# Turning the local-attention gates by a transposing DMA instead of on TensorE, in a hybrid retention and sliding-window layer

## The chip, the cores and the metric

The kernel runs on one core of one Trainium2 chip. The metric is the device time of one execution in microseconds (us). Before the change it is 714.54 us, the median of three runs (714.14 to 716.06).

## The reference

One layer of a decoder, for one sequence of 2048 tokens with 1024 channels, all in float32. One input projection gives the queries, keys, values and gates of two groups of heads: a retention (four heads, in chunks of 128 tokens) and a sliding-window softmax attention (eight heads, window 128). Each group's output is multiplied by SiLU of its gate, the two are put side by side and projected back:

```python
def reference(x, norm_w, w_in, ret_norm_w, q_norm_w, k_norm_w, sinks, rel_bias, w_out):
    h = rms_norm(x, norm_w).astype(x.dtype)
    proj = jnp.einsum('bsd,de->bse', h, w_in).astype(jnp.float32)
    rq, rk, rv, rg, sq, sk, sv, sg = jnp.split(proj, offsets, axis=-1)
...
    ro = ro * jax.nn.silu(rg)
...
    so = so * jax.nn.silu(sg)
    mixed = jnp.concatenate([ro, so], axis=-1).astype(x.dtype)
    x = x + jnp.einsum('bse,ed->bsd', mixed, w_out)
```

What matters here is the gating, `so * silu(sg)`, and that its result is the stationary operand of the output projection, for which it must lie with the channels on the partitions.

## The kernel before, in words

The 2048 tokens are 16 chunks of 128, taken as eight pairs `p` of an even chunk (row 0) and an odd chunk (row 1). Every projection is done as one level of a Strassen-like scheme: the input is cut into quarters (two rows of tokens, two halves of the inner dimension), and seven products `m` = 1 to 7 of sums and differences of quarters give the four quarters of the result. So there are four stages, each of 7 x 8 products: two for the queries, keys and values, one for the gates (`W3`, `B3`, L1421 to L1423), one for the output projection (`W4`, `B4`, L1424 to L1426). A product is 12 matmuls of 128 x 512, because each operand is split into a high part that TensorE's fast float32 mode keeps whole and a low rest (`split`, L493: the high part by ScalarE, the rest by VectorE): high by high, high by low, low by high, for four slices of the inner dimension.

The products of a stage go in the order of `STEPS` (L67): m = 1 and 2, then 6, then 5, then 7 and 4, then 3, over groups of two pairs in the gate stage and of three pairs in the last stage (`TWOS`, `THREES`). When products are finished, parts of the result come out (`products`, L671): m = 2 gives row 0, first column half; m = 4 gives row 1, first half; m = 7 gives row 1, second half; m = 3 gives row 0, second half. In the gate stage the first column half is the retention's gate, the second the local attention's. So the local attention's gates of odd chunks come out with m = 7 (tile `r`), those of even chunks with m = 3, at the very end of that stage (tile `t`).

Each of them goes to `gate` (L1323). ScalarE makes SiLU of it. For the retention (`n == 0`) VectorE multiplies the group's output `go` by the gate, TensorE turns the product in four 128 x 128 pieces against the identity into a PSUM bank (`turn gated`, L1348 to L1352), and ScalarE copies it back. For local attention (`n == 1`), whose output lies turned in DRAM already, VectorE multiplies the gate `g` by the softmax's reciprocal sums, TensorE turns the gate itself in four pieces, and VectorE multiplies the bank by `go` (`mixed`). The result stands in `mixes`, from which `blocks` (L597) makes the operands of the last stage: quarters 0 and 1 for m = 1 and 2, all four for m = 6 and later.

Nothing is issued in the order of the text. Every step is handed to a planner (`Program`, L134) with a cost for each engine that can take it, the buffers that it needs, and a due time counted in products (one unit is 12 matmuls). The planner emits for each engine a fixed order, and the program runs in it: an engine that comes to an instruction whose input isn't there waits, and what is queued behind it waits too. All loads and stores are issued by SP's queue, also in one fixed order. Tiles of 128 x 512 float32 come from one pool of 93 (`CAP`), with a limit for each use (`SHARE`); of the eight PSUM banks, three at a time are for the running products of a stage.

Of the kernel before, what the change touches and what calls it, by code (L numbers as in the profile page):

```python
# [29 lines left out]
F32 = mybir.dt.float32  # L30
F32R = mybir.dt.float32r
I32 = mybir.dt.int32
AF = mybir.ActivationFunctionType
ALU = mybir.AluOpType
PSUM = bass.MemoryType.PSUM
# [3 lines left out]
P = 128  # L39
# [16 lines left out]
CAP = {"k": 93, "h": 6, "bank": 8}  # L56
SMALL, COUNTS = 3, {"ms": 1, "rxt": 1, "rqk0t": 1, "rqk1t": 1}

SHARE = {"x": 8, "raw": 38, "acc": 21, "wr": 20, "wh": 20, "att": 34, "ret": 14, "rin": 14, "gate": 4, "mix": 34, "norm": 6, "res": 6, "first": 5, "block": 3, "rest": 6}

AHEAD_OF = {"x": 3.0, "wh": 8.0}

# [15 lines left out]
FOURS, THREES, TWOS = Turns(4), Turns(3), Turns(2)  # L78
# [55 lines left out]
class Program:  # L134
# [5 lines left out]
    def op(self, cost, go, r=(), w=(), due=0.0, table=None, label="", also=()):  # L140

        o = Op()
        o.cost, o.go, o.due, o.after, o.set, o.label = cost, go, due, [], table, label
        o.n, o.left, o.ready, o.end, o.seen, o.by = len(self.ops), 0, 0.0, 0.0, 0.0, None
        deps = set()
        for b in r:
            if b.writer is not None:
                deps.add(b.writer)
        for b in w:
            if b.writer is not None:  # L150
                deps.add(b.writer)
            deps.update(b.readers)
        for b in r:
            b.readers.append(o)
        for b in w:
            b.writer, b.readers = o, []
        o.bufs = list(dict.fromkeys((*r, *w, *also)))
        for b in o.bufs:
            b.left += 1
        o.new = [b for b in (*w, *also) if b.ap is None and b.tag]  # L160
        for d in deps:
            if d is not o:
                d.after.append(o)
                o.left += 1
        self.ops.append(o)
        return o
# [146 lines left out]
def dve(n, two=False, lat=0.08):  # L313
    return (0.067 + n / 960, 0.067 + n / 960 + lat, two)


def act(n, more=0.0):
    return (0.094 + n / 1200 + more, 0.2 + n / 1200 + more, False)
# [6 lines left out]
def both(n):  # L325
    return {"V": dve(n, True)}
# [16 lines left out]
def turns(count):  # L343
    t = 0.109 * count
    return {"T": (t, t + 0.25, False)}
# [34 lines left out]
def layer(ctx, tc, xt, xfirst, xtok, nw, w_in, w_rn, qkw, sinks, biasg, rope, dmask, gpow, w_out, out):  # L380
    nc = tc.nc
    order = Order(tc)
    V, G, A, Q, T = (Engine(order, e) for e in (nc.vector, nc.gpsimd, nc.scalar, nc.sync, nc.tensor))
# [16 lines left out]
    op = prog.op  # L400

    def kb(name, share, dtype=F32):
        return Buf("k", None, dtype, name, share)
# [7 lines left out]
    def ps(share="rest", name="m"):  # L411
        return Buf("bank", None, F32, name, share)
# [8 lines left out]
    def given(ap):  # L421
        return Buf(ap=ap)
# [4 lines left out]
    def load(b, src, due, kbytes=256, to=lambda t: t, cost=None, also=(), of=lambda t: t):  # L427
        op(
            cost or dma(kbytes), lambda e: e.dma_start(to(b()), of(src())), [src], [b], due, label=f"load {b.name}",
            also=also,  # L430
        )

    def store(dst, b, due, kbytes=256, of=lambda t: t):
        op(dma(kbytes), lambda e: e.dma_start(dst(), of(b())), [b], [dst], due, label=f"store {b.name}")
# [4 lines left out]
    ident = fixed([P, P], "ident")  # L439
    nw_sb = fixed([P, KT], "nw_sb")  # L440
    wr = fixed([P, 4], "wr")
# [155 lines left out]
    def blocks(src, base, seq, keep):  # L597


        B, held = {}, {}  # L600
        for m, p in seq.all:
            due = base + seq.at[m, p]
            if m in (1, 2):
                late = keep and m == 1 and p < OPENING
                held[m, p] = src(p, m - 1, base + seq.first[6] - 8 + 1.4 * p if late else due - 3)
                if late:
                    continue
            elif m == 6:
                soon = base + seq.first[6] - 4 + 1.4 * p
                a11, a21, a22 = held[1, p], src(p, 2, soon - 4), src(p, 3, soon - 4)  # L610
                s1 = held[5, p] = combine(a21, a22, ALU.add, 512, soon, None, "raw", "x")
                s2 = held[6, p] = combine(s1, a11, ALU.subtract, 512, soon, None, "raw", "x")
                held[7, p] = combine(a11, a21, ALU.subtract, 512, due + 2, a21)
                held[3, p] = combine(held[2, p], s2, ALU.subtract, 512, due + 2, held[2, p])
                held[4, p] = a22
                if keep:
                    for i, k in enumerate((5, 6, 7, 3)):
                        store(keep[i][p], held[k, p], base + seq.at[k, p] + 1)
            B[m, p] = split(held[m, p], 512, due - 0.6, "x", "x")
        return B  # L620
# [48 lines left out]
    turn = Buf(name="turn", ap=())  # L669
# [90 lines left out]
    def last_product(x, w, d, t, p):  # L760

        (xh, xl), n = x, 256
        for i in range(2):
            acc, c = ps("block", "acc"), slice(i * n, (i + 1) * n)
            for k in range(4):
                wh, wl = w[k]

                def go(e, acc=acc, c=c, wh=wh, wl=wl, k=k):
                    for j, (a, b) in enumerate(((xh, wh), (xh, wl), (xl, wh))):
                        e.matmul(  # L770
                            acc()[:, :n], a()[:, k * P : (k + 1) * P], b()[:, c], start=(k == j == 0),
                            stop=(k == 3 and j == 2),
                        )

                op(f32r(n, 3), go, [xh, xl, wh, wl], [acc, turn], d, label="product 3")
            r = Part(t, lambda t, c=c: t[:, c])
            op(
                {"V": dve(n)}, lambda e, r=r, acc=acc: e.tensor_tensor(r(), acc()[:, :n], r(), ALU.add), [acc, t], [r],
                d - 3, label="add t", also=(t,),
            )  # L780
            store(given(out[2 * p, :, 512 + i * n : 512 + (i + 1) * n]), r, d + 1, 128)

    def spill(to, n):
        def sink(p, row, col, b, due):
# [535 lines left out]

    mixes = {}

    def gate(n, c, due, g):  # L1323


        o, pm = kb("go", "mix"), ps()
        load(o, (ro_dram, so_dram)[n][c], due - 4)
        op(
            {"A": act(512, 0.09)},
            lambda e: e.activation(g(), g(), AF.Silu, scale=rstd_all()[:, c : c + 1]),  # L1330
            [g, rstd_all], [g], due - 1, "silu", label="silu",
        )
        if n == 0:
            op(
                both(512), lambda e: e.tensor_tensor(o(), o(), g(), ALU.mult), [g, o], [o], due,
                label="gate",
            )
        else:

            def go(e):  # L1340
                gv = g().rearrange("p (m g d) -> p m g d", g=KVH, d=HD)
                rden = rden_all[c]().rearrange("p (m g) -> p m g", g=KVH).unsqueeze(3)
                e.tensor_tensor(gv, gv, rden.to_broadcast([P, GRP, KVH, HD]), ALU.mult)

            op(both(512), go, [g, rden_all[c]], [g], due, label="gate")
        t = o if n == 0 else g

        def go(e):  # L1348
            for i in range(4):
                e.transpose(pm()[:, i * P : (i + 1) * P], t()[:, i * P : (i + 1) * P], ident())  # L1350

        op(turns(4), go, [t, ident], [pm], due + 0.3, "small", label="turn gated")  # L1352
        if n == 0:
            op({"A": act(512)}, lambda e: e.activation(o(), pm(), AF.Copy), [pm], [o], due + 0.4, label="mixed")
        else:
            op(
                {"V": dve(512)}, lambda e: e.tensor_tensor(o(), pm(), o(), ALU.mult), [pm, o], [o],
                due + 0.4, label="mixed",
            )
        mixes[c // 2, c % 2 * 2 + n] = o  # L1360

    def gates(p, row, col, b, due):

        c = 2 * p + row
        if row == col == 0:
            store(g_dram[p], b, due)
            g = kb("g", "gate")
            due = GATE[0] + p * GATE[1]
            load(g, g_dram[p], due - 4)
            gate(0, c, due, g)  # L1370
        else:
            gate(col, c, max(due, GATE[0]) + 0.5, b)


    def residual(p, row, col, due):
        res = kb("res", "res")
        load(res, given(xtok[2 * p + row, :, col * 512 : (col + 1) * 512]), due - 4)
        return res

    def result(p, row, col, b, due):  # L1380
        store(given(out[2 * p + row, :, col * 512 : (col + 1) * 512]), b, due + 1)


    make_identity(nc, ident())
# [5 lines left out]
    def go(e):  # L1390
# [10 lines left out]
        label="no values",  # L1401
# [20 lines left out]
    B3 = kept_blocks(2 * n7, TWOS)  # L1422
    products(B3, W3, 512, 2 * n7, TWOS, gates)  # L1423
    W4 = weights(w_out, 0, 512, (wr, 4), 3 * n7, THREES)  # L1424
    B4 = blocks(lambda p, q, due: mixes[p, q], 3 * n7, THREES, None)
    products(B4, W4, 512, 3 * n7, THREES, result, residual)  # L1426
    prog.emit()
    layer.time = prog.time
# [4 lines left out]
WIN = (54.0, 5.6)  # L1433
RET = (107.0, 2.8)
GATE = (150.0, 1.2)


_SHAPES = {
# [93 lines left out]
```

## Time and profile before

| | |
|---|---|
| median of three runs | 714.54 us |
| the profiled execution's own time | 714.56 us |
| its span, first to last instruction | 712.9 us |
| TensorE busy (PE) | 708.2 us, 99% |
| TensorE weight loads (PEld) | 610.1 us, 86% |
| VectorE busy (DVE) | 605.5 us, 85% |
| ScalarE busy (ACT) | 439.4 us, 62% |
| DMA traffic | 153.48 MB, 215 GB/s on the mean |
| granted TensorE clock | 1.00 |

The span leaves out 1.66 us of the execution's own time (714.56 - 712.9). The table's shares are means over the whole span; the stages differ, and the gates are turned between about 496 and 562 us. A row of the chain in order of time gives a start, a duration, an engine, the tile that is written and a count. A row of groups gives the line (here always L376, the helper that records every operation, so groups are told apart by their tiles), engine, operation, tiles written and read, their shapes, the count, the busy time in us and the mean of one in ns. Durations of neighbours on one engine overlap a little: a ScalarE instruction that is listed with 0.62 us is followed by the next 0.52 us after its start.

### The profile page before, as it was taken

What the parts mean: (1) busy time and instruction counts of PE and PEld (TensorE: products, weight loads), DVE (VectorE), ACT (ScalarE), POOL (GpSimd) and SP (SyncE); (2) the same over time, 40 slices, a digit from 0 to 9 for tenths busy, and PEclk for the clock granted to TensorE, in tenths of its full rate; (3) what the DMA queues carried; (4) which work ended last, traced back from release to release, by engine and by line L of the source; (5) the groups of instructions that cost most, each with busy time, mean ns of one, the idle gap of its engine ahead of it and who ended that gap; (6) DMA issues with size and microseconds to landing.
All of it is one profiled execution on the core that took longest, in us unless ns stands there. A gap on an engine that the chain in (4) does not pass through costs nothing.

```text
span 712.9 us, 15364 instructions
## 1 busy us (share of the span) xinstructions
PE 708.2 (99%) x5388; PEld 610.1 (86%) x5388; DVE 605.5 (85%) x1456; ACT 439.4 (62%) x1073; POOL 42.9 (6%) x75
## 2 busy tenths in 40 slices
PE   9999999999999999999999999999999999999998
PEld 7888888889999999998888888888888888888886
DVE  6999887887997977799999979997899997677762
ACT  8566966655895548777587767778975336321500
POOL 1000000025110001001000010000000000000000
PEclk9999999999999999999999999999999999999999
DMA  9979938977645567989966648593971422323722
GB/s 327 351 262 305 401 121 301 323 235 248 188 149 182 163 206 223 366 274 303 309 217 227 203 157 267 168 369 101 312 245 42 161 76 74 97 80 122 263 98 94
DMA packets 102029, 153.48 MB, mean 215 GB/s; under 512 B 11840, under 2 KB 40512, under 8 KB 101952
## 3 DMA queue, kind: packets, MB, share of 16 engines
q1 hardware_dynamic: 101808, 152.49, 64.0%
q8 instruction: 43, 0.70, 0.4%
q14 instruction: 34, 0.28, 0.1%
q10 hardware_dynamic: 144, 0.00, 0.0%
HBM read 110.44 MB, written 42.01 MB: 214 GB/s over the span
## 4 chain that ended last, share of the span: by engine, by line
PE 99%; DVE 0%; issue 0%
PE acc L376 81%; PE m L376 18%; DVE t L376 0%; DVE none L376 0%
## 5 line engine op out<-in xcount | busy, mean ns | idle before, releaser
L376 PE MATMUL acc<-w,x 128*128 128x512 f32 (+1 forms) x2700 | 600.2, 379 | 0.0
L376 PEld LDWEIGHTS acc<-w,x 128*128 128x128 f32 x2700 | 490.5, 188 | 78.7 <-issue 2.7
L376 DVE TENSOR_TENSOR x<-x 128x512 fp32r<-128x512 f32 (+2 forms) x220 | 145.9, 684 | 16.2 <-ACT x L376 15.2
L376 ACT ACTIVATE x<-x 128x512 fp32r<-128x512 f32 (+1 forms) x187 | 111.5, 615 | 13.0 <-PE acc L376 10.0
L376 DVE TENSOR_TENSOR w<-w 128x512 fp32r<-128x512 f32 (+3 forms) x96 | 62.4, 671 | 2.8 <-ACT w L376 2.7
L376 DVE TENSOR_TENSOR s<-acc,s 128x512 f32<-128x512 f32 (+1 forms) x64 | 42.1, 657 | 24.4 <-PE acc L376 23.9
L376 ACT ACTIVATE w<-w 128x512 fp32r<-128x512 f32 (+1 forms) x72 | 40.7, 599 | 24.5 <-DMA w<-in_w_out 18.3
L376 ACT ACTIVATE pm<-lg,nm 128x128 f32<-128x128 f32 x128 | 49.7, 392 | 6.7 <-DVE lg L376 6.7
L376 DVE CUSTOM_DVE_ANT_0 lg<-m,bias,nsnk 128x160 f32<-128x160 f32 x128 | 42.4, 383 | 10.1 <-PE m L376 10.0
L376 DVE SCALAR_TENSOR_TENSOR w<-w,nw_sb 128x512 fp32r<-128x512 f32 (+3 forms) x72 | 49.5, 707 | 0.4 <-ACT w L376 0.2
L376 POOL TENSOR_SCALAR_AFFINE_SELECT own<-pT 64x512 f32<-64x512 f32 x32 | 25.6, 813 | 292.5 <-ACT pT L376 239.5
L376 ACT ACTIVATE x<-go 128x512 fp32r<-128x512 f32 x40 | 23.7, 624 | 24.5 <-PE acc L376 21.3
L376 ACT ACTIVATE s<-acc 128x512 f32<-128x512 f32 (+1 forms) x32 | 18.2, 567 | 31.5 <-PE acc L376 27.1
L376 DVE TENSOR_TENSOR t<-acc,t 128x512 f32<-128x512 f32 (+2 forms) x33 | 21.1, 641 | 16.0 <-PE acc L376 15.8
L376 DVE TENSOR_TENSOR r<-acc,t 128x512 f32<-128x512 f32 (+1 forms) x32 | 21.0, 656 | 10.3 <-PE acc L376 10.2
L376 ACT ACTIVATE w<-w,nw_sb 128x512 fp32r<-128x512 f32 (+3 forms) x43 | 28.0, 681 | 1.7 <-DMA nw_sb<-in_nw 1.2
L376 DVE TENSOR_TENSOR x<-go,x 128x512 fp32r<-128x512 f32 x40 | 27.4, 688 | 0.0
L376 DVE TENSOR_TENSOR t<-acc,s 128x512 f32<-128x512 f32 (+1 forms) x32 | 21.0, 658 | 6.7 <-PE acc L376 6.3
L376 ACT ACTIVATE ro<-ro,nmu,rg 128x128 f32<-128x128 f32 x64 | 25.1, 482 | 0.9 <-DVE nmu L376 0.9
L376 ACT ACTIVATION_READ_ACCUMULATOR pm<-lg,nm 128x1 f32 x128 | 24.3, 190 | 0.0
L376 ACT ACTIVATE c<-acc 128x512 f32<-128x512 f32 (+1 forms) x24 | 13.4, 559 | 16.6 <-PE acc L376 13.7
L376 ACT ACTIVATE xk<-xk 128x512 f32<-128x512 f32 x32 | 19.8, 618 | 5.2 <-DMA xk<-in_xtok 5.2
(132 smaller groups left out, 704.6 us busy)
## 6 DMA issues: line engine op xcount, KB each, us to landing
x<-in_xt SPq DMA_DIRECT2D x80, 256.0 KB, 4.8
x<-s_dram SPq DMA_DIRECT2D x64, 256.0 KB, 4.2
w<-in_w_in SPq DMA_DIRECT2D x40, 256.0 KB, 5.1
s_dram<-x SPq DMA_DIRECT2D x32, 256.0 KB, 5.1
xk<-in_xtok SPq DMA_DIRECT2D x32, 256.0 KB, 5.2
res<-in_xtok SPq DMA_DIRECT2D x32, 256.0 KB, 3.0
w<-in_w_out SPq DMA_DIRECT2D x20, 256.0 KB, 3.5
aq<-aq_dram SPq DMA_DIRECT2D x16, 256.0 KB, 4.6
```

The lines of the kernel that those rows point to most:

```text
L376: return lambda *a, **k: self.order.put(op(*a, **k))
```

## The change

The gate of local attention is no longer turned by TensorE. ScalarE copies the 512 float32 of each partition, seen as 1024 words of 16 bits, into a new tile `apart` in which the low and the high halves stand in two planes; one transposing DMA, issued on SP's queue, turns all eight 128 x 128 pieces of 16 bits into a new tile `turned`; ScalarE puts the planes together again in the gate's own tile; and VectorE multiplies that by `go`, from SBUF instead of PSUM. The retention's gates are turned on TensorE as before. Besides, the last stage takes the odd chunk as its first row (`q ^ 2`, with the residual and the output rows swapped to match), so that the even chunks' gates, which come out last, are first needed at m = 6 and not at m = 2; and the due times of the odd and even gates are put `LEAD` = 12 units ahead of that need. The new tiles have a limit of 6 together (`SHARE`).

```diff
+    def turn_by_dma(t, due):
+        apart, turned = kb("apart", "turned"), kb("turned", "turned")
+        words = lambda x: x.bitcast(U16).rearrange("p (c h) -> p h c", h=2)
+        planes = lambda x: x.bitcast(U16).rearrange("p (h c) -> p h c", h=2)
+        op(
+            {"A": act(1024)}, lambda e: e.activation(planes(apart()), words(t()), AF.Copy), [t], [apart], due,
+            label="apart",
+        )
+        op(
+            {"Q": (1.4, 3.0, 0.45)},
+            lambda e: e.dma_start_transpose(
+                turned().bitcast(U16).rearrange("p (j r) -> p j r", r=P), apart().bitcast(U16)
+            ),
+            [apart], [turned], due, label="turn by dma",
+        )
+        op(
+            {"A": act(1024)}, lambda e: e.activation(words(t()), planes(turned()), AF.Copy), [turned], [t], due + 0.1,
+            label="together",
+        )
...
-        t = o if n == 0 else g
-
-        def go(e):
-            for i in range(4):
-                e.transpose(pm()[:, i * P : (i + 1) * P], t()[:, i * P : (i + 1) * P], ident())
-
-        op(turns(4), go, [t, ident], [pm], due + 0.3, "small", label="turn gated")
         if n == 0:
+            pm = ps()
+
+            def go(e):
+                for i in range(4):
+                    e.transpose(pm()[:, i * P : (i + 1) * P], o()[:, i * P : (i + 1) * P], ident())
+
+            op(turns(4), go, [o, ident], [pm], due + 0.3, "small", label="turn gated")
             op({"A": act(512)}, lambda e: e.activation(o(), pm(), AF.Copy), [pm], [o], due + 0.4, label="mixed")
         else:
-            op(
-                {"V": dve(512)}, lambda e: e.tensor_tensor(o(), pm(), o(), ALU.mult), [pm, o], [o],
-                due + 0.4, label="mixed",
-            )
+            turn_by_dma(g, due + 0.3)
+            op(both(512), lambda e: e.tensor_tensor(o(), g(), o(), ALU.mult), [g, o], [o], due + 0.4, label="mixed")
...
-            gate(col, c, max(due, GATE[0]) + 0.5, b)
+            need = 3 * n7 + (THREES.at[1 + col, p] if row else THREES.first[6] - 4 + 1.4 * p)
+            gate(col, c, max(due + 0.5, GATE[0] + 0.5, need - LEAD), b)
...
-        load(res, given(xtok[2 * p + row, :, col * 512 : (col + 1) * 512]), due - 4)
+        load(res, given(xtok[2 * p + 1 - row, :, col * 512 : (col + 1) * 512]), due - 4)
...
-        store(given(out[2 * p + row, :, col * 512 : (col + 1) * 512]), b, due + 1)
+        store(given(out[2 * p + 1 - row, :, col * 512 : (col + 1) * 512]), b, due + 1)
...
-    B4 = blocks(lambda p, q, due: mixes[p, q], 3 * n7, THREES, None)
+    B4 = blocks(lambda p, q, due: mixes[p, q ^ 2], 3 * n7, THREES, None)
...
+LEAD = 12.0
```

How the change moves instructions: on TensorE, the end of the gate stage before. `go`, `r` and `t` name the tile that is turned (the retention's gated output, the local attention's odd and even gates), `acc<-w,x` are the matmuls of the products.

```order
L376 MATMUL m<-ident,t 128x128 x4
L376 MATMUL acc<-w,x 128x512 x18
L376 MATMUL m<-ident,t 128x128 x4
L376 MATMUL acc<-w,x 128x512 x9
L376 MATMUL m<-ident,t 128x128 x4
L376 MATMUL acc<-w,x 128x512 x6
L376 MATMUL m<-ident,t 128x128 x4
L376 MATMUL acc<-w,x 128x512 x15
L376 MATMUL m<-ident,t 128x128 x4
L376 MATMUL acc<-w,x 128x512 x18
L376 MATMUL m<-ident,t 128x128 x4
L376 MATMUL acc<-w,x 128x512 x636
```

The same place on TensorE with the change:

```order
L377 MATMUL m<-ident,go 128x128 x8
L377 MATMUL acc<-w,x 128x512 x12
L377 MATMUL m<-ident,go 128x128 x8
L377 MATMUL acc<-w,x 128x512 x48
L377 MATMUL m<-ident,go 128x128 x4
L377 MATMUL acc<-w,x 128x512 x12
L377 MATMUL m<-ident,go 128x128 x4
L377 MATMUL acc<-w,x 128x512 x12
L377 MATMUL m<-ident,go 128x128 x4
L377 MATMUL acc<-w,x 128x512 x48
```

All 64 turns of `r` and `t` are gone (eight gates of each, four pieces a gate), and with them the breaks that they made in the products: between the last local-attention values and the long run that ends the program there are 23 separate groups of turns before and 13 with the change. The 64 turns of `go` stay.

On ScalarE with the change, around the last three of the sixteen turns, at the beginning of the last stage (`apart` and `turned` are the new tiles, `s<-acc` empties a bank of a product, `x<-go` makes a high part):

```order
L377 ACTIVATE apart_8301<-t_6893 128x1024
L377 ACTIVATE apart_8317<-t_6938 128x1024
L377 ACTIVATE apart_8327<-t_7073 128x1024
L377 ACTIVATE t_6859<-turned_8291 128x2x512
L377 ACTIVATE s_8352<-acc_8320 128x512
L377 ACTIVATE x_8358<-go_7667 128x512
L377 ACTIVATE x_8365<-go_7700 128x512
L377 ACTIVATE t_6893<-turned_8311 128x2x512
L377 ACTIVATE s_8380<-acc_8348 128x512
L377 ACTIVATE x_8385<-go_7732 128x512
L377 ACTIVATE t_6938<-turned_8342 128x2x512
L377 ACTIVATE s_8404<-acc_8374 128x512
```

Before, none of the `apart` and `turned` rows stand there. Each of the second kind waits for its DMA, and the emptying of a product's bank stands right behind it in ScalarE's order.

On SP's queue with the change, in the gate stage's second half, the transposing DMAs stand among the loads of the output projection's weights, of `go` and of the residual `res`:

```order
L377 DMA_TRANSPOSE turned<-apart 128x8x128
L377 DMA go<-so_dram 128x512 x2
L377 DMA w<-in_w_out 128x512 x3
L377 DMA_TRANSPOSE turned<-apart 128x8x128
L377 DMA w<-in_w_out 128x512
L377 DMA go<-so_dram 128x512 x2
L377 DMA res<-in_xtok 128x512
L377 DMA_TRANSPOSE turned<-apart 128x8x128
L377 DMA res<-in_xtok 128x512
```

Each waits for ScalarE's `apart`, and the loads behind it with it.

More of the change, by code (lines that the diff above doesn't have):

```diff
@@ L32 @@
 I32 = mybir.dt.int32
+U16 = mybir.dt.uint16
 AF = mybir.ActivationFunctionType
@@ L57 @@
 SMALL, COUNTS = 3, {"ms": 1, "rxt": 1, "rqk0t": 1, "rqk1t": 1}
-SHARE = {"x": 8, "raw": 38, "acc": 21, "wr": 20, "wh": 20, "att": 34, "ret": 14, "rin": 14, "gate": 4, "mix": 34, "norm": 6, "res": 6, "first": 5, "block": 3, "rest": 6}
+SHARE = {"x": 8, "raw": 38, "acc": 21, "wr": 20, "wh": 20, "att": 34, "ret": 14, "rin": 14, "gate": 4, "mix": 34, "norm": 6, "res": 6, "turned": 6, "first": 5, "block": 3, "rest": 6}
 AHEAD_OF = {"x": 3.0, "wh": 8.0}
@@ L780, in last_product @@
             )
-            store(given(out[2 * p, :, 512 + i * n : 512 + (i + 1) * n]), r, d + 1, 128)
+            store(given(out[2 * p + 1, :, 512 + i * n : 512 + (i + 1) * n]), r, d + 1, 128)
     def spill(to, n):
@@ L1321, in layer @@
     mixes = {}
+    def turn_by_dma(t, due):
[17 more added lines that the diff above has]
+        )
     def gate(n, c, due, g):
-        o, pm = kb("go", "mix"), ps()
+        o = kb("go", "mix")
         load(o, (ro_dram, so_dram)[n][c], due - 4)
```

## The prediction

> **What bounds the kernel now.** I read the page first: busy times, then the chain that ended last.
>
> ```profile
> PE 708.2 (99%) x5388; PEld 610.1 (86%) x5388; DVE 605.5 (85%) x1456; ACT 439.4 (62%) x1073; POOL 42.9 (6%) x75
> ...
> PE 99%; DVE 0%; issue 0%
> PE acc L376 81%; PE m L376 18%; DVE t L376 0%; DVE none L376 0%
> ```
>
> The chain is TensorE nearly alone. Then the waits of TensorE, which have a single row:
>
> ```profile
> PE m L376 <- DVE none L376: 1.3, 1, 1.3
> ```
>
> After its first 1.3 us it never waits. So each microsecond taken out of its stream shortens the program, as long as the others keep feeding it; and each wait that is put into it lengthens the program in full. The question is thus asked in two parts: what leaves TensorE, and whether ScalarE, VectorE and the DMAs can still keep up where the gates are turned. For the first, the chain in order of time at that place (start, duration, count):
>
> ```profile
> 495.93 3.06 PE m L376 x28
> ...
> 509.04 1.75 PE m L376 x16
> 510.78 4.11 PE acc L376 x18
> 514.89 0.44 PE m L376 x4
> 515.33 3.46 PE acc L376 x15
> ...
> 538.20 0.44 PE m L376 x4
> 538.64 3.45 PE acc L376 x15
> ```
>
> A group of four turns holds TensorE for 0.44 us, and larger groups cost the same per turn: 3.06 / 28 and 1.75 / 16 are both 0.109 us. For the second part, three windows (columns: length, then the busy time of PE, PEld, DVE, ACT, POOL with counts, clock, DMA share, GB/s):
>
> ```profile
> 494.00:576.00 82.00, 82.00 (x437) 68.50 (x428) 77.59 (x131) 50.61 (x93) 0.00 (x0) 1.00 0.58 190
> 515.00:593.00 78.00, 78.00 (x378) 64.61 (x376) 77.75 (x129) 38.73 (x68) 0.00 (x0) 1.00 0.40 135
> 593.00:620.00 27.00, 27.00 (x121) 22.37 (x120) 17.61 (x29) 14.68 (x27) 0.00 (x0) 1.00 0.23 75
> ```
>
> VectorE is full from 515 to 593 us, with 9.4 us to spare right behind; ScalarE has 31.4 us to spare in 82. It is that spare time that the change uses.
>
> **TensorE's part.** The 64 turns of `r` and `t` go. The groups by tile, with all their busy time:
>
> ```profile
> L376 PE MATMUL m<-ident,t 128*128 128x128 f32 x32 | 4.8, 272 | 0.0
> L376 PE MATMUL m<-ident,r 128*128 128x128 f32 x32 | 4.5, 272 | 0.0
> ```
>
> These 9.3 us share some time with neighbouring products, so I take the chain's price: 64 x 0.109 = 7.0 us. Breaks cost a little besides. In a run without any, a matmul costs 150.81 / 663 = 0.2275 us:
>
> ```profile
> 5.04 150.81 PE acc L376 x663
> ```
>
> Fifteen of them make 3.41 us; behind a break they took 3.46 and 3.45, so a break costs about 0.03 to 0.04. Ten breaks fewer (23 to 13): 0.3 us. Together 7.3 us. It could be 7.0 if breaks are free, or 7.7 with 0.07 each.
>
> **VectorE's part.** The multiplication by `go` reads SBUF in place of PSUM. The old form, and one that reads SBUF alone:
>
> ```profile
> L376 DVE TENSOR_TENSOR go<-m,go 128x512 f32<-128x512 f32 x16 | 10.9, 687 | 0.1
> L376 DVE TENSOR_TENSOR go<-go,s 128x512 f32<-128x512 f32 x8 | 5.5, 687 | 2.2 <-ACT s L376 2.2
> ```
>
> 687 ns either way: nothing. VectorE gets no more work, but its full stretch now has 7.3 us less of TensorE's time beside it. What covers this is work done ahead, and the 9.4 us that it has free from 593 to 620.
>
> **ScalarE's part.** It gets 32 copies of 1024 words. No such copy is in the trace; the nearest rows are a plain copy of two sizes, and two of them in a row:
>
> ```profile
> L376 ACT ACTIVATE w<-w 128x512 fp32r<-128x512 f32 x56 | 33.0, 622 | 24.5 <-DMA w<-in_w_out 18.3 <-PE acc L376 3.3 <-DVE res L376 1.5
> L376 ACT ACTIVATE w<-w 128x384 fp32r<-128x384 f32 x16 | 7.7, 518 | 0.0
> ...
> 562.50 1.14 ACT L376 ACTIVATE x<-go 128x512 fp32r<-128x512 f32 x2
> ```
>
> 128 elements more cost 104 ns, so 1024 take 622 + 416 = 1038 ns; and an instruction holds ScalarE 0.10 us less than it is listed with (1.14 - 0.62 = 0.52), which gives 0.94 us. Strided words of 16 bits could cost more, at most twice as I bound it, or less, not under the 0.52 of one 512-element copy. I take 0.94, since I see no reason why a lane would need two steps for a word. In all 32 x 0.94 = 30 us.
>
> Where does it lie? In ScalarE's order with the change, 12 of the `apart` and 13 of the `together` copies stand between the last attention outputs (494 us before) and the fourth emptied bank of the last stage (576 us before): 25 x 0.94 = 23.5 us. ScalarE's 50.6 us become 74.1, in a window that shrinks from 82.0 to 74.7. It fits, with 0.6 us left. (At twice the price per copy it would be 97.6, some 23 us too much; I count that end with the slow rival below, which it resembles.) What it waits for there (490 to 620 us) decides the rest:
>
> ```profile
> ACT x L376 <- PE acc L376: 19.4, 8, 4.8
> ACT s L376 <- PE acc L376: 12.3, 8, 2.3
> ACT t L376 <- DVE t L376: 11.4, 7, 2.4
> ```
>
> The first two are waits because it is ahead of TensorE; these just shrink. The third is a wait for VectorE in the middle of the gates, and if it stayed whole, ScalarE would fall behind. What it may fall behind by, before TensorE notices, is shown by the first product of the last stage, of which these are the low part on VectorE and the emptied bank on ScalarE:
>
> ```profile
> 547.27 0.69 DVE L376 TENSOR_TENSOR x<-go,x 128x512 fp32r<-128x512 f32 x1
> ...
> 559.26 0.60 ACT L376 ACTIVATE s<-acc 128x512 f32<-128x512 f32 x1 [0.81 <-PE acc L376]
> ```
>
> That product ended at about 559.2 and took 12 x 0.2275 = 2.73 us, so it began at 556.5, 8.5 us after its operand was ready. The other limit is the banks: three for running products, so one may be emptied two products late, 5.4 us. I use the smaller, 5.4 us, as the cushion, and take ScalarE's part as hidden.
>
> **The DMAs' part.** Sixteen transposing DMAs of 256 KB. None is in the trace. Rows of that size, from issue to landing:
>
> ```profile
> xk<-in_xtok SPq DMA_DIRECT2D x32, 256.0 KB, 5.2
> ...
> w<-in_w_out SPq DMA_DIRECT2D x20, 256.0 KB, 3.5
> ...
> out<-t SPq DMA_DIRECT2D x7, 256.0 KB, 2.0
> ```
>
> So 2.0 to 5.2 us if a transposing DMA goes like a plain one; up to 10.4, twice the slowest, if not (a rival). I take 3.5, the row of the loads that run in the same stretch. A page of the Trainium skill says the same: by "Advanced Engine Details and Errata", section X-Bar Transpose (TRN2), such DMAs are as fast as plain ones; by that the sum stands as it is. But the table DGE: Hardware vs Software of that page calls transposing less efficient when the hardware path makes the descriptors, as SP's queue does, and gives no figure.
>
> What is late if the DMA is slow: ScalarE stands at the `together` copy, in order. The shortest cover is for the gate `t_6893`: between its `apart` and its `together` stand two `apart`, one `together`, one emptied bank and two high parts, 3 x 0.94 + 0.50 + 2 x 0.52 = 4.36 us of work. Counted alike, the last eight have 5.6 us on the mean, four others 7.6 to 12.9, the first four over 20. Against 3.5 us all are covered.
>
> The issue costs SP little; it mostly waits, as when it needs 22.5 us for five loads whose buffers aren't free:
>
> ```profile
> 521.54 0.38 SPq L376 DMA_DIRECT2D x<-s_dram  x1
> ...
> 530.46 22.50 SPq L376 DMA_DIRECT2D res<-in_xtok  x5
> ```
>
> Sixteen issues of 0.38 are 6 us among such waits. Behind a transposing DMA that waits for its `apart` stand loads of `w_out`, `go` and `res`; in the order these come early enough that I charge nothing. As for bandwidth, 135 GB/s at a share of 0.40 is 338 GB/s at full share, so 256 KB take 0.78 us and sixteen 12.4 us, a share of 0.16 more; even twice that leaves room.
>
> **The swapped rows and the due times** cost nothing: the same loads, stores and products with other indices. They put off the first need of the `t` gates from m = 2 to m = 6, thirteen products or 35 us later for the first pair. That is what makes room for the longer way.
>
> **The sum.** 714.56 - 7.3 = 707.3 us, from the profiled execution's own time, which is within 0.02 us of the median of the runs, so 707.3 stands for the median too.
>
> **The rivals.**
>
> *ScalarE becomes the bound for a while.* For it: 74.1 of 74.7 us, and the 11.4 us of waits for `t`. Against it: the due times spread the `t` gates into the last stage, where it is half free. If all 11.4 stay, it is 85.5 - 74.7 = 10.8 us late, 5.4 beyond the cushion: 712.7. If half of that loss happens, 2.7 us: 710.0, my figure for this rival.
>
> *The transposing DMA is slow (the other side).* Beyond the covers above, ScalarE waits in order at each `together`, with the banks and high parts of the last stage behind it. At 10.4 us the last eight wait 8 x 4.8 = 38.4 us and the other four 3.5; since two or three are in flight together and share a wait, I take half, 21 us; less the cushion of 5.4 that is 15.6 us on TensorE: 707.3 + 15.6 = 722.9. It decides from about 8.6 us on, where loss and gain are equal (half of 24 to 25 us, less 5.4, is about 7). For it speaks that one instruction moves 1024 words of each row in eight pieces to other partitions, unlike any row here; against it only the likeness to plain DMAs. The Trainium skill's "VectorE: DVE Perf Modes", section The three transpose paths, gives 1309 ns for one 128 x 128 piece by DMA against 390 on TensorE; eight of these in a row would be, as an estimate from that page, 10.5 us, and the time by it about 723. The trace has TensorE's turn at 0.109 us in a stream, well under that page's figure.
>
> *The gain is eaten up.* A DMA of 8 to 9 us, or the worst end of the first rival: about 713 to 715, no change.
>
> **How the numbers follow.** Forecast (706.4 to 709) 0.55; ScalarE as the bound (709 to 712.7) 0.21; eaten up 0.09; slow DMA 0.15. About 0.3%, or 2.1 us, is what a measurement of this kernel can tell from no change: faster is below 712.4, slower above 716.7. Faster takes the forecast and nearly all of the first rival: 0.74. Within 0.3%: 0.11, with a little of both ends. Slower: 0.15. The range begins at 706.4, the sum with 7.7 us and a run 0.4 us below the median as the fastest shown was; it goes to 715.0, which takes in the first rival and most of the third, about 0.83 in all.
>
> **What would show it.** The groups of turns of `r` and `t` are gone and TensorE's waits still have one row: right. The `apart` and `together` copies near 1.04 us: right; near 2 us, ScalarE's sum is wrong. The transposing DMA's issue to landing at 3 to 5 us: right; from 8.6 us on, with waits of ScalarE for `turned` and of TensorE for ScalarE or VectorE near 560 to 600 us, the slow DMA has won. Waits of TensorE there while `turned` is never waited for speak for the first rival.

## The result, and the profile after

With the change the kernel takes 709.76 us (median of six runs, 709.27 to 710.77); the kernel before took 714.89 us beside it (714.14 to 716.06). The ratio is 0.9926, with a 95% interval from 0.9914 to 0.9939: 5.1 us less. The sum had 7.3 us. So the sign and the range held, 2.2 us of the gain are missing, and the time lies 0.8 us outside what the prediction called its forecast (706.4 to 709). The profiled execution took 709.88 us, its span is 708.0.

First the page of the kernel after: busy times, then the chain that ended last.

```profile
PE 702.2 (99%) x5324; PEld 603.3 (85%) x5324; DVE 606.9 (86%) x1458; ACT 471.9 (67%) x1103; POOL 43.8 (6%) x75
...
PE 97%; DVE 2%; issue 0%; DMA 0%; SPq 0%; ACT 0%
```

TensorE has 64 instructions and 6.0 us less, ScalarE 32.5 us more, where 30 were forecast. The chain, which was TensorE's alone, now has 2% of VectorE in it. TensorE's waits show where (us in total, times, the longest):

```profile
PE m L377 <- DVE none L377: 1.3, 1, 1.3
PE acc L377 <- DVE x L377: 0.8, 1, 0.8
PE acc L377 <- ACT x L377: 0.2, 1, 0.2
```

The first row stood there before; the other two are new. In TensorE's timeline they lie a little way into the last stage (start, busy time, count; the time idle before it in brackets):

```profile
555.31 16.60 PE L377 MATMUL acc<-w,x 128*128 128x512 f32 x72
572.12 9.26 PE L377 MATMUL acc<-w,x 128*128 128x512 f32 x38 [0.22 <-ACT x L377]
582.17 122.39 PE L377 MATMUL acc<-w,x 128*128 128x512 f32 x550 [0.80 <-DVE x L377]
```

The two stops cost 1.0 us by name. From 555.31 us to the end of the second stop, at 582.17, are 26.86 us for 110 matmuls. In the run e5 below the same 660 matmuls go without a stop in 147.31 us; less the 122.39 us of the last 550, that leaves 24.92 us for these 110. So this stretch lost 1.9 us, most of the 2.2 us by the medians: behind each stop the next few matmuls start late as well. Compared start by start with e5, TensorE falls back 0.8 us around the first stop and 1.1 us around the second. Single executions differ elsewhere too: the run of 660 begins 0.8 us later here than in e5 (554.49 us), and that difference arises in the first 27 us, far from the gates.

Which engine was short of time there? The windows, of the length that the prediction used and of 82 us (length, then PE, PEld, DVE, ACT, POOL, clock, DMA share, GB/s):

```profile
494.00:568.70 74.70, 74.70 (x387) 61.98 (x378) 64.20 (x112) 73.77 (x115) 0.00 (x0) 1.00 0.95 276
494.00:576.00 82.00, 81.73 (x415) 67.14 (x406) 70.24 (x121) 80.19 (x123) 0.00 (x0) 1.00 0.94 270
...
515.00:593.00 78.00, 76.94 (x359) 63.00 (x358) 73.18 (x122) 69.42 (x101) 0.00 (x0) 1.00 0.78 218
```

ScalarE has 0.9 us free in 74.7, and still only 1.8 in 82: it is full past the end of the window for which its work was counted. VectorE, full from 515 to 593 us before, now has 4.8 us to spare there, because it waits for others. The DMA share went from 0.58 to 0.94 in the second window.

Next, the groups of the new copies on ScalarE (busy, mean of one in ns, idle before them):

```profile
L377 ACT ACTIVATE r<-turned 128x1024 uint16<-128x1024 uint16 x8 | 11.3, 1407 | 0.1
L377 ACT ACTIVATE t<-turned 128x1024 uint16<-128x1024 uint16 x8 | 11.1, 1387 | 0.0
L377 ACT ACTIVATE apart<-t 128x1024 uint16<-128x1024 uint16 x8 | 8.5, 1080 | 0.1
L377 ACT ACTIVATE apart<-r 128x1024 uint16<-128x1024 uint16 x8 | 8.4, 1067 | 0.1
```

Taking apart costs what was forecast (1.07 us against 1.04 listed). Putting together costs 1.40, a third more. And the tile `turned` (its DMAs' time on SP in ns, who waited for it, and the time from issue to landing):

```profile
L377 SPq DMA_TRANSPOSE turned<-apart x16: 1232/1321/1889, 508.6 to 571.3; - x16
...
who waited for it (us, times):
  DVE x L377: 1.9, 1
  DVE go L377: 1.0, 2
  ACT s L377: 0.8, 1
...
DMA to landing us min/median/max: 3.0/4.4/5.8
```

A transposing DMA lands after 4.4 us where 3.5 was taken, and holds SP for 1.3 us where 0.38 was taken. Three groups wait for it, 3.7 us in all. The longest wait, 1.9 us, is VectorE's and ends at 576.62 us, between the two stops.

### The profile page after: what moved, and what is told of

It is laid out like the page before. It is cut to its first block, busy times and chain, and to the rows that moved or that the text cites. A ratio compares the mean times of both kernels' runs of the same rounds, so it can differ in the third digit from the quotient of the medians.

```text
span 708.0 us, 15295 instructions
## 1 busy us (share of the span) xinstructions
PE 702.2 (99%) x5324; PEld 603.3 (85%) x5324; DVE 606.9 (86%) x1458; ACT 471.9 (67%) x1103; POOL 43.8 (6%) x75
## 4 chain that ended last, share of the span: by engine, by line
PE 97%; DVE 2%; issue 0%; DMA 0%; SPq 0%; ACT 0%
PE acc L377 80%; PE m L377 17%; DVE w L377 1%; DVE x L377 1%; DVE t L377 0%; DMA res<-in_xtok 0%; DVE res L377 0%; DVE go L377 0%; SPq L377 0%; ACT x L377 0%; DVE none L377 0%
## 5 line engine op out<-in xcount | busy, mean ns | idle before, releaser
L377 DVE TENSOR_TENSOR r<-acc,t 128x512 f32<-128x512 f32 (+1 forms) x32 | 21.0, 656 | 11.8 <-PE acc L377 11.4
```

What stands on the lines that cost most here:

```text
L377: return lambda *a, **k: self.order.put(op(*a, **k))
```

## The experiments

Three theories of the missing 2.2 us were put to the test. **A**: ScalarE, because "putting together" costs more than was counted. **B**: the transposing DMA, which lands later and holds SP longer. **C**: VectorE by itself, whose output `x` TensorE waits for by name. Each kernel was timed with the kernel before beside it; the times are medians, with the 95% interval of the ratio to that kernel before.

### One part made cheap: e1, e2, e3, e4

**e1** writes the joined words in a row instead of with a stride:

```diff
-            {"A": act(1024)}, lambda e: e.activation(words(t()), planes(turned()), AF.Copy), ...
+            {"A": act(1024)}, lambda e: e.activation(pairs(t()), together(turned()), AF.Copy), ...
```

Here `pairs` and `together` are the views `"p (c h) -> p c h"` of the target and `"p (h c) -> p c h"` of the planes.

> The change with one edit: the copy that puts the planes together goes through the words in their order, so that it writes without a stride and reads the two planes in turn. The order of all instructions stays. Theory A (the shortfall of 2.4 us against the sum comes from ScalarE, because this copy holds it 1.22 us and not 0.94): the copy falls from 1.38 to about 1.06 us, 16 x 0.3 = 4.8 us leave ScalarE's full stretch, and the time falls from 709.8 to 707.6 to 708.4. Theory B (it comes from the transposing DMA, which holds SP's queue 1.32 us and lands after 4.4, so that ScalarE and VectorE wait in order for it): no change, 709.5 to 710. Theory C (VectorE is full there whatever the others do): no change either. If the copy's time depends on the reading side instead, it doesn't fall and this run tells nothing.

It took 708.38 us (708.04 to 708.68), 0.9911 of the kernel before (0.9898 to 0.9925): by the medians 1.4 us less than the change, by the ratios 1.1 us, and the intervals of the two ratios overlap. The copies in it, in the view of groups, and TensorE's last rows:

```profile
L377 ACT ACTIVATE r<-turned 128x1024 uint16<-128x1024 uint16 x8 | 9.5, 1184 | 0.0
L377 ACT ACTIVATE t<-turned 128x1024 uint16<-128x1024 uint16 x8 | 9.4, 1180 | 0.0
```

```profile
554.46 25.38 PE L377 MATMUL acc<-w,x 128*128 128x512 f32 x110
581.04 122.40 PE L377 MATMUL acc<-w,x 128*128 128x512 f32 x550 [1.20 <-DVE x L377]
```

Each copy is 0.2 us shorter, 3.4 us less work on ScalarE, and the first stop is gone. So A is part of the cause. But the stop for VectorE's `x` has grown from 0.80 to 1.20 us, and by this one execution the 110 matmuls lose 581.04 - 554.46 - 24.92 = 1.7 us where the change lost 1.9. What A is worth by itself stays open, between these 0.3 us and the 1.4 us of the medians.

**e2** replaces the transposing DMA by a plain one between the same two tiles, and leaves the 32 copies:

```diff
-            lambda e: e.dma_start_transpose(
-                turned().bitcast(U16).rearrange("p (j r) -> p j r", r=P), apart().bitcast(U16)
-            ),
+            lambda e: e.dma_start(turned().bitcast(U16), apart().bitcast(U16)),
```

The local attention's gates stay unturned in it, so it shows a time and not a kernel to use.

> The change with the transposing DMA replaced by a plain DMA of the same 256 KB from the same tile to the same tile; the local attention's gates are left unturned, so the output is another one. The order of all instructions stays. Theory B: SP's issue falls from 1.32 to about 0.4 us and the landing from 4.4 to 2 to 4, the waits for the turned tile at 569 to 577 us go, and the time falls to 707.6 to 708.5. Theories A and C: 709.3 to 710.

It took 708.41 us (707.58 to 708.87), ratio 0.9911 (0.9897 to 0.9924): by the medians again 1.4 us less than the change, with intervals that overlap. The tile `turned`, the window of 82 us and TensorE's last rows in it:

```profile
L377 SPq DMA_DIRECT2D turned<-apart x16: 470/471/553, 508.5 to 569.9; - x16
...
who waited for it (us, times):
  DVE go L377: 1.0, 2
...
DMA to landing us min/median/max: 2.3/2.5/5.4
```

```profile
494.00:576.00 82.00, 81.49 (x407) 67.24 (x400) 71.51 (x122) 80.54 (x125) 0.00 (x0) 1.00 0.77 270
```

```profile
555.04 17.05 PE L377 MATMUL acc<-w,x 128*128 128x512 f32 x74
572.60 130.55 PE L377 MATMUL acc<-w,x 128*128 128x512 f32 x586 [0.51 <-DVE x L377]
```

The same 256 KB need 2.5 us instead of 4.4, and 0.47 us of SP instead of 1.32; two of the three groups that waited for `turned` are gone. For the same 270 GB/s the DMA engines are busy 0.77 of the window instead of 0.94. Now the second stop is gone and the one at 572 us is left; the loss is 572.60 - 555.04 = 17.56 us less the 147.31 - 130.55 = 16.76 us that these 74 matmuls need, 0.8 us. So B is part of the cause too, and by this one execution the larger part, though ScalarE is as full as ever (80.54 of 82). How it reaches TensorE can be read from VectorE's wait of 1.9 us for `turned`: the change and e1 have it, and the stop near 582 us behind it; e2, e5, e8, e10 and e11 have neither.

**e3** turns only the odd chunks' gates by DMA, the even ones on TensorE as before; **e4** turns all of them on TensorE and keeps the swapped rows and the due times:

```diff
-        if n == 0:
+        if n == 0 or not (c % 2 == 1):     # e3; in e4 the bracket is False
```

> Only the odd chunks' gates are turned by DMA, the even ones on TensorE as before; the rows stay swapped and the due times as in the change. By the sum half of 7.3 us, so 711.2 if nothing is lost. Theories A and B put the loss into the last eight turns at the beginning of the last stage (even gates): then 711.0 to 711.6 here. If the loss lies in the odd gates, 712.5 or more.

> All gates turned on TensorE as before; only the swapped rows and the later due times are kept. By the prediction's sum these cost and bring nothing: 714.4 to 715.3, as the kernel before. If the later due times alone load the beginning of the last stage so that TensorE waits, it is slower by 1 us or more, and part of the shortfall is theirs and not the DMA's.

e3 took 710.9 us (710.6 to 711.32), ratio 0.9947 (0.9934 to 0.9961): 3.5 us less than the kernel before, where half of the sum is 3.65. No loss is seen in that half, and TensorE has no new wait. e4 took 714.65 us (714.32 to 715.52), ratio 1.0003 (0.9995 to 1.0012): the swap and the due times by themselves do nothing, as forecast.

### Both cheap, the other half, no swap, true prices: e5, e7, e6, e8

**e5** is e1 and e2 together, so its gates stay unturned too.

> Both earlier edits at once: the planes are put together with whole words written (1.18 us instead of 1.38) and the DMA is a plain copy, which leaves the local attention's gates unturned. The order of all instructions stays. Each edit alone took off 1.4 us. If the shortfall against the sum is what ScalarE and the DMA hold up together, it ends here: 707.0 to 707.7, the sum's 707.3 against the runs of before, and no wait of TensorE but the first. If VectorE's full stretch keeps a part of its own, the time stays at 708.0 or above, with waits of TensorE for VectorE's low parts left.

It took 706.99 us (706.78 to 708.4), ratio 0.9901 (0.9887 to 0.9914, which just meets the change's 0.9914), 7.4 us less than the kernel before. TensorE's waits, and its last run:

```profile
PE m L377 <- DVE none L377: 1.3, 1, 1.3
```

```profile
554.49 147.31 PE L377 MATMUL acc<-w,x 128*128 128x512 f32 x660
```

The wait for VectorE's `x` is gone although VectorE has the same work, and the last 660 matmuls run without a stop. So the full sum of 7.3 us was there to be had; what ate 2.2 of it is A and B together. C falls: VectorE was named because it came last, not because it was short of time.

**e7** turns only the even chunks' gates by DMA (`c % 2 == 0` in the line of e3).

> Only the even chunks' gates are turned by DMA, the odd ones on TensorE as before; swap and due times as in the change. The odd half alone took off 3.6 us, all that the sum gives it. If the loss belongs to the even gates themselves (short covers in ScalarE's order at the beginning of the last stage), this half takes off only about 1.5 us of its 3.65: 712.5 to 713.2. If the loss comes from the sum of both halves on ScalarE, this half alone is free too: 710.6 to 711.2.

It took 711.57 us (710.84 to 711.85), ratio 0.996 (0.9947 to 0.9972): 2.8 us less than the kernel before, against 3.65. The interval holds 3.65 too, so whether the even half loses something by itself stays open; its profile has no new wait of TensorE. The two halves alone gained 3.5 and 2.8, together 6.3; the change gained 5.1. So some 1.2 us of the loss belong to both halves at once, though with these intervals that is a hint.

**e6** undoes the swap and the due times and keeps the turning by DMA:

```diff
-    B4 = blocks(lambda p, q, due: mixes[p, q ^ 2], 3 * n7, THREES, None)
+    B4 = blocks(lambda p, q, due: mixes[p, q], 3 * n7, THREES, None)
...
-            gate(col, c, max(due + 0.5, GATE[0] + 0.5, need - LEAD), b)
+            gate(col, c, max(due, GATE[0]) + 0.5, b)
```

> The DMA turn alone: the even chunk is the output's first row again, and the due times are those of before. The even gates, which come out last, are then needed at m = 2. If the swap is what gives the longer way its time, TensorE waits near the beginning of the last stage and the gain shrinks further or turns around: 711 to 718. If the planner finds room without it, 709.5 to 710.5 as with the change.

It took 729.16 us (728.63 to 729.27), ratio 1.0207 (1.0193 to 1.0221), slower than anything I had expected. TensorE's waits:

```profile
PE acc L377 <- ACT x L377: 10.6, 1, 10.6
PE m L377 <- DVE go L377: 3.0, 2, 2.4
PE acc L377 <- DVE x L377: 2.4, 3, 1.4
```

The longest ends at 570.08 us. What ScalarE did until then, in its timeline:

```profile
557.66 0.60 ACT L377 ACTIVATE s<-acc 128x512 f32<-128x512 f32 x1 [2.00 <-DMA turned<-apart]
558.16 1.35 ACT L377 ACTIVATE t<-turned 128x1024 uint16<-128x1024 uint16 x1
559.37 1.03 ACT L377 ACTIVATE apart<-t 128x1024 uint16<-128x1024 uint16 x1
560.31 2.52 ACT L377 ACTIVATE t<-turned 128x1024 uint16<-128x1024 uint16 x2
...
564.20 2.52 ACT L377 ACTIVATE t<-turned 128x1024 uint16<-128x1024 uint16 x2
...
568.23 1.33 ACT L377 ACTIVATE t<-turned 128x1024 uint16<-128x1024 uint16 x1
569.43 0.60 ACT L377 ACTIVATE x<-go 128x512 fp32r<-128x512 f32 x1
```

The even gates are needed by the first products here, and ScalarE puts six of them together before it makes the high part that TensorE waits for. It is one chain in order: DMA, ScalarE's copies, the high part. The edit isn't pure: the planner also moved the last attention values behind this place, so the 14.8 us over the kernel before aren't all the price of a missing swap. That the swap, free by itself (e4), is what makes room for the long way is shown in kind, not in size.

**e8** is e1, with the planner told the measured prices: 0.1 us more for the copy, and 1.3 us of SP for the DMA instead of 0.45. The computation is complete.

```diff
-            {"Q": (1.4, 3.0, 0.45)},
+            {"Q": (1.4, 3.0, 1.3)},
...
-            {"A": act(1024)}, lambda e: e.activation(words(t()), planes(turned()), AF.Copy), ...
+            {"A": act(1024, 0.1)}, lambda e: e.activation(pairs(t()), together(turned()), AF.Copy), ...
```

> A version that is meant to be used: whole words written, and the planner is told the measured prices (putting together 1.05 us in place of 0.95, 1.3 us of SP's queue for each transposing DMA in place of 0.45), so that its order leaves more room. If the remaining loss is only a matter of the fixed order being planned on too low prices, 707.2 to 708.0; if the DMA's landing or VectorE keep it, 708.4 as with whole words alone.

It took 707.65 us (707.18 to 708.08), ratio 0.9906 (0.9892 to 0.9919), 0.7 us less than e1 by the medians, with intervals that overlap. But TensorE has only its first wait left, and its last 660 matmuls take 147.31 us as in e5. The DMAs are transposing ones as in the change:

```profile
494.00:576.00 82.00, 82.00 (x397) 68.04 (x393) 71.38 (x120) 78.32 (x124) 0.00 (x0) 1.00 0.97 270
```

Their share is even higher (0.97), but TensorE doesn't stop. So the slow DMAs are harmless where the order allows for them.

### How far ahead, and the prices alone: e9, e10, e11

**e9** and **e10** are e8 with `LEAD` at 16 and at 10 products instead of 12; **e11** is the change with nothing but the measured prices told (`act(1024, 0.28)`, and 1.3 for the DMA).

> The version with whole words and measured prices, with LEAD 16 instead of 12: the even gates are turned up to four products (11 us) earlier, into the end of the gate stage. If the loss is a matter of short covers in ScalarE's order, longer covers help or leave it: 707.2 to 707.8 against 707.65. If it is ScalarE's and VectorE's load, which is higher at the end of the gate stage, more of it there makes the time longer: 708.5 or more.

> The same with LEAD 10: the even gates are turned up to two products (5.5 us) later, nearer to their need at m = 6. Short covers: longer than 707.65 by some tenths or more. Load: the same or less, 707.0 to 707.7.

> The change with nothing but the measured prices told to the planner (1.23 us for putting together, 1.3 us of SP's queue); the copy itself still writes strided words, 1.38 us. If the loss is a matter of an order planned on too low prices, this alone brings most of it back: 707.5 to 708.3 against the change's 709.8. If the copy's real time is what counts, 709 to 710.

e9 took 710.63 us (710.03 to 711.53), ratio 0.9942 (0.993 to 0.9955); e10 707.22 (707.08 to 708.01), ratio 0.9895 (0.9882 to 0.9909). More time ahead makes it slower, less does not. By the medians e10 is the fastest kernel here that does the whole computation; the intervals of e8 and e11 overlap with its own. Two windows of e9, then the same of e10:

```profile
494.00:550.00 56.00, 56.00 (x278) 46.49 (x279) 44.49 (x76) 55.67 (x92) 0.00 (x0) 1.00 0.96 279
550.00:575.00 25.00, 22.88 (x93) 18.10 (x93) 24.21 (x41) 22.70 (x33) 0.00 (x0) 0.93 0.81 218
```

```profile
494.00:550.00 56.00, 56.00 (x277) 46.35 (x275) 45.83 (x80) 54.95 (x92) 0.00 (x0) 1.00 0.99 299
550.00:575.00 25.00, 25.00 (x116) 20.69 (x115) 22.89 (x38) 21.33 (x31) 0.00 (x0) 1.00 0.79 215
```

With the longer lead ScalarE has 0.33 us free up to 550 and is behind after it, and TensorE waits 2.1 us there (22.88 of 25), 1.8 of them in one stop for ScalarE's `x`; with the shorter one it has 1.05 us free and TensorE waits for nothing. The two profiled executions are further apart, 711.2 and 707.25 us. Most of the rest fits the granted clock: 0.93 on the mean of that window, 0.50 from 561.3 to 563.3 us, and 25 x 0.07 is about 1.8 us. If the covers between a DMA and its use had been too short, e9 would have been the faster one. In e9 it is work that ScalarE can't fit in that costs time, and starting it earlier only moved it to where ScalarE is fuller.

e11 took 707.59 us (707.06 to 709.58), ratio 0.9895 (0.988 to 0.9911). Its copies are the dear ones of the change, its DMAs the slow ones, its computation complete, and by the medians all of the 2.2 us are back; its interval ends just where the change's begins (0.9911 and 0.9914). Its runs spread, the slowest reaching the change's, so the size is uncertain. But its profile is of that slowest execution (709.58 us), and even there the last 660 matmuls take 147.31 us without a stop; TensorE's new waits, 0.6 and 0.3 us, lie in the attention, before 331 us. So the loss in the last stage came from a fixed order that had been made with prices too low. Two prices were told at once; which of them mattered isn't shown.

## Why the prediction was right or wrong, point by point

- **TensorE's part, 7.3 us: right.** e5 and e10, in which TensorE has only its first wait, gained 7.4 and 7.9 us against the kernel before beside them (714.37 and 715.08). The chain's price of 0.109 us a turn was the one to take; the difference to 9.3 us of listed busy time is overlap. The price of a break was read a little low: 3.46 and 3.45 less 3.41 are 0.04 to 0.05 us, not 0.03 to 0.04, which makes ten breaks 0.4 to 0.5 us; nothing else hangs on it.
- **Swap and due times, nothing: right** (e4, 1.0003). That they make room for the long way was right in kind (e6).
- **VectorE's part, nothing: right.** In e5 its wait is gone with the same work.

- **ScalarE's part: one of two steps that failed.** The prediction said "It fits, with 0.6 us left" and took "ScalarE's part as hidden". Its price was right for `apart` and wrong for `together`, as these rows of ScalarE's timeline show:

```profile
562.74 1.38 ACT L377 ACTIVATE t<-turned 128x1024 uint16<-128x1024 uint16 x1
563.96 0.63 ACT L377 ACTIVATE x<-go 128x512 fp32r<-128x512 f32 x1
...
570.95 0.60 ACT L377 ACTIVATE s<-acc 128x512 f32<-128x512 f32 x1 [0.83 <-DMA turned<-apart]
```

  The next instruction begins 1.22 us after the copy, not 0.94: 16 x 0.28 = 4.5 us more in all, in a window with 0.6 us left. That the measured 73.77 us agree with the forecast 74.1 is no success, since an engine can't show more than a window holds; what didn't fit stood behind 568.7 us, and it is between there and 582 that TensorE stopped.
- **The DMAs' part: the other one.** The prediction had "Against 3.5 us all are covered" and charged nothing for SP. 4.4 us is just over the 4.36 that was called the shortest cover, and 1.32 us of SP for 0.38 makes 15 us more of SP in that stretch. What waited longest was VectorE's `x` (1.9 us), and in the last row above the emptying of a bank, not the `together` copy that the prediction had watched; that `x` and `s` stand in the place of an `apart` which the DMA was still reading is my reading of it, not shown. The DMA share from 515 to 593 us was to rise by 0.16, at most twice that; it rose from 0.40 to 0.78, and with the plain DMAs of e2 to 0.59.
- **What made a loss of the two: the order.** In e11 the copies are as dear and the DMAs as slow, and its last stage doesn't stop. So the two cost 1.9 us in an order that was planned with 0.95 us for the copy and 0.45 us of SP for the DMA, and nothing there in one planned with 1.23 and 1.3.
- **What the Trainium skill says of such DMAs.** The prediction cited the Trainium skill, "Advanced Engine Details and Errata", section X-Bar Transpose (TRN2), by which such DMAs are as fast as plain ones. The runs disagree, 4.4 us against 2.5 in e2. That page's table DGE: Hardware vs Software, which the prediction set against it, compares the hardware path with the software path; no run here shows that, since SP's queue issued all the transposing DMAs.
- **The rivals.** The result, 709.76, lies on the first rival's figure of 710.0, and a full ScalarE is half of what the runs showed. That the figure fits is luck: it lived on 11.4 us of waits for VectorE's `t`, and these are gone; the DMA, which it left out, has its own part in the loss; and its sign, that `turned` is never waited for, wasn't met (3.7 us). The range held because it was wide enough to take in this rival and no change at all. ScalarE's waits after the change, 490 to 620 us, now have other names:

```profile
ACT w L377 <- DVE w L377: 13.2, 4, 7.8
...
ACT s L377 <- DMA turned<-apart: 0.8, 1, 0.8
```

  The slow DMA, from 8.6 us on, did not come: the slowest landing was 5.8 us.

What stays open: how much of the DMA's share in the loss is SP's 1.3 us an issue and how much the landing at 4.4 us, since e2 took both away; what ScalarE's copies cost by themselves, between 0.3 and 1.4 us (e1); which of the two told prices mattered in e11; and whether the even half loses anything alone.

## What to carry to other kernels

When work is moved to an engine that then has under 1% of a window free, prices that are too low show in the result (here 2.2 of 7.3 us, by a copy priced a quarter too low and a DMA that held its queue over three times as long as was taken): measure the form of each instruction by itself before counting it as hidden. If the order is fixed by a planner, tell it the measured prices first: here that alone brought back most of the loss (e11), while more time ahead made it worse (e9). And a wait goes by the name of what came last: TensorE waited for VectorE's `x`, but it was ScalarE's copies and the DMA that had to be made cheaper, or planned at their price.

## What the runs showed of the hardware that was not expected

- Which side of a ScalarE copy is strided matters. With 1024 words of 16 bits: strided read and planes written in a row 1.07 us; planes read in a row and strided write 1.40; planes read by turns and written in a row 1.18. The last form does the same work as the second.
- A transposing DMA makes many small packets. The page's count after, then in e2 with plain ones:

```profile
DMA packets 118924, 157.66 MB, mean 223 GB/s; under 512 B 28736, under 2 KB 57408, under 8 KB 118848
```

```profile
DMA packets 104332, 157.66 MB, mean 223 GB/s; under 512 B 12096, under 2 KB 40768, under 8 KB 104256
```

  The bytes are the same, with 16,640 more packets under 512 B, 1040 for each of the sixteen. At shares of 0.94 and 0.77 over 82 us, each costs (0.94 - 0.77) x 82 / 16 = 0.87 us more of all 16 engines.
- After a stop of TensorE the granted clock can fall; the long one in e6 shows it. TensorE's row behind it, and the windows of the stop and of what follows:

```profile
570.08 1.22 PE L377 MATMUL acc<-w,x 128*128 128x512 f32 x2 [10.56 <-ACT x L377]
```

```profile
559.50:570.10 10.60, 0.04 (x2) 0.02 (x1) 6.56 (x10) 10.15 (x14) 0.00 (x0) 0.75 0.96 216
570.10:573.00 2.90, 2.60 (x5) 1.65 (x6) 2.90 (x6) 2.88 (x3) 0.00 (x0) 0.50 0.00 0
```

  The clock was 0.50 in the next 2.9 us, and two matmuls took 1.22 us where two of an unbroken run take 0.45. In e9 one stop of 1.81 us, with 0.31 us more behind it, was followed by 0.50 from 561.3 to 563.3 us; behind the stop of 1.20 us in e1 the clock stayed at 1.00. Such a wait costs more than its length.
